# Stored remainders of the projection weights, and three split out-projection tiles used once more at each change of pass

## The chip, the cores and the metric

One Trainium2 chip, of which the program uses one core. The metric is the device time of one execution in microseconds (us), and less is better. Times are given beside the rows of the profile they come from. The engines are named as in the profile: PE (TensorE, matrix products), PEld (its weight loads), DVE (VectorE), ACT (ScalarE), POOL (GpSimd) and SP (SyncE, which issues most of the DMAs).

## What is computed

One layer of a hybrid decoder on 1024 tokens of width 1024, in float32:

```python
def reference(x, ...):
    h = rms_norm(x, norm_mix)                       # (1024, 1024)
    proj = h @ w_in                                 # 1024 -> 8 x 1024
    xa, ga, q, f, v, g, m_a, m_b = split(proj)
    y_a = rg_lru(conv(xa), ...) * gelu(ga)          # recurrence over time
    y_b = rms_norm(hgrn2(q, f, v), hg_norm) * silu(g)   # 8 heads, chunked
    y = sigmoid(m_a) * y_a + sigmoid(m_b) * y_b
    x = x + y @ w_out                               # out-projection, 1024 -> 1024
    h = rms_norm(x, norm_mlp)
    x = x + square(relu(h @ w_up)) @ w_down         # 1024 -> 4096 -> 1024
    return rms_norm(x, norm_final)
```

## The kernel before

**Products in three passes.** The operands of the large products are kept as two float32r tiles, a high part H (the value cast to float32r) and a remainder L (the value minus H). `mm3` (lines 131 to 136) issues three matmuls for each product: H by H, H by L and L by H. For a weight tile, `split` (lines 87 to 90) makes both parts: ACT casts `raw` to `wH` (line 89), then DVE subtracts and writes `wL` (line 90).

**How a weight tile gets to PE.** `seq` is a list, made ahead, of all weight tiles in the order in which PE uses them. Each is 128x1024 floats, 512 KB. `load_w` has SP load tile i into one of 4 `raw` buffers (line 97); `split_w` takes two of the 6 buffers with the tag `w` (three pairs H and L), so that a new pair can only be written when PE is through with a pair used earlier. `next_w` hands out the next tile and has two more split ahead of it (`ahead=2`).

**Mixer projections (about 10 to 550 us).** The 1024 tokens are worked through in two halves of 512 (`c` = 0 and 1), and in each half in 4 pairs of heads (`p` = 0 to 3): 8 stages. A stage uses 9 tiles of weights (two each for v, xa and q, two for f, one, called rg, for the gates of the recurrence). The same 36 tiles of w_in and of the gates are thus loaded and split once in the first half and once more in the second: `pair_tiles` has 72 entries. Between the projections PE computes the chunked attention of the pair before (`hgrn`): scores `sc`, transposes `pk` of the keys `kk`, products `pkv`, and outputs `po`. The order of PE in this part is fixed by the program (`pin`); DVE and ACT are ordered by a scheduler that the framework runs when the program is built, in which `tc.high_priority` moves the splits ahead.

**Gates (about 550 to 835 us).** The four gate projections for all tokens, each as one Strassen-like product of 7 steps. Nothing here is touched.

**Out-projection (about 835 to 930 us).** w_out is 8 tiles: 0 to 3 for output columns 0 to 511 (`hf` = 0), 4 to 7 for columns 512 to 1023 (`hf` = 1). It is gone through three times: `out_proj(0, ...)` for the first 512 tokens, 24 matmuls a tile and four in `pp`; then the loop `for part in range(2)` for the next two lots of 256 tokens, 12 matmuls a tile. So `seq` holds the 8 tiles three times. In the same time the second norm runs (`second_norm`): for each of 8 blocks of 128 tokens ACT squares and sums a row block (line 155), DVE adds (line 156), POOL takes the power (line 157), DVE scales to `xn_h` (line 158), PE transposes it (`xT_h`, line 1203), ACT copies it back (line 1204), and ACT and DVE split the operands `h2...` of the MLP. Late in it, `first_weights` and the code behind it load and split the first weights of the MLP (`q`, `s`, `wA`, `ws10`, `wA120`, `ws30`). The last pass is pinned on PE, and the first MLP products (`uX`) stand between its last transposes.

**MLP (about 930 us to the end).** Untouched.

The names that the prediction uses: `raw<-wts_in` is the load of a weight tile, `wH<-raw` its cast on ACT, `wL<-raw,wH` its subtraction on DVE; `kk<-kk,seg` is the last DVE step before the transposes `pk`; `pv` is the product with v, whose two weight tiles the loop `v_steps` uses by turns from its first token block on; `x2s<-po,x2s` adds a finished out-projection block to the residual.

Of the kernel before, what the change touches and what calls it, by code (L numbers as in the profile page):

```python
# [10 lines left out]
F32 = mybir.dt.float32  # L11
# [7 lines left out]
P = 128  # L19
# [3 lines left out]
NC = S // T  # L23
# [8 lines left out]
MIX_TILES = NPAIR * N_PAIR_TILES  # L32
OUT_TILES = 8
# [13 lines left out]
def trunk(ctx: ExitStack, tc: tile.TileContext, x, wts, mlp, pv, gains, mask_f, mask_u, out):  # L47
    nc = tc.nc
    V, A, G, PE = nc.vector, nc.scalar, nc.gpsimd, nc.tensor
# [4 lines left out]
    dram = ctx.enter_context(tc.tile_pool(name="dram", bufs=1, space=DRAM))  # L54
# [8 lines left out]
    def bank(tag, name):  # L63
        return ps.tile([P, 512], F32, tag=tag, name=name, bufs={"pj": 4, "sc": 2, "hg": 2}[tag])


    pair_tiles = []
    for i in range(NC * NPAIR):
        at = (0, 1, 2, 3, 4, 6, 5)
# [3 lines left out]
    seq = [wts[i] for i in pair_tiles]  # L73
    seq += [mlp[2 * QUADS + q, h] for q in range(2) for h in range(2)]
    n_mix = len(seq)
    for c in range(NC + 1):
        seq += [wts[MIX_TILES + j] for j in range(OUT_TILES)]
    most = [n_mix]
    ready, made = {}, [0]


    in_order = [True]
# [1 line left out]
    def keep(ins):  # L84
        if in_order[0]:
            tc.keep_in_program_order(ins)

    def split(src, h, lo):
        keep(A.copy(h, src))  # L89
        keep(V.tensor_tensor(out=lo, in0=src, in1=h.bitcast(F32), op=ALU.subtract))  # L90
# [4 lines left out]
    def load_w(i):  # L95
        raw = raw_tile(f"raw{i}")
        nc.sync.dma_start(raw, seq[i])
        return raw

    def split_w(i, raw):  # L100
        h = wp.tile([P, 1024], F32R, tag="w", name=f"wH{i}", bufs=6)
        lo = wp.tile([P, 1024], F32R, tag="w", name=f"wL{i}", bufs=6)
        with tc.high_priority(400):
            split(raw, h, lo)
        return h, lo

    raws = []

    def fill_w(n):
        while made[0] < min(n, most[0]):  # L110
            i = made[0]
            raw = raws.pop(0) if raws else load_w(i)
            ready[made[0]] = split_w(i, raw)
            made[0] += 1

    def get_w(i, ahead=2):
        fill_w(i + ahead + 1)
        return ready.pop(i)

    used = [0]  # L120

    def next_w():
        used[0] += 1
        return get_w(used[0] - 1)

    pinned = [False]

    def pin(ins):
        if pinned[0]:
            tc.keep_in_program_order(ins)  # L130

    def mm3(o, ah, al, bh, bl, first, last, goes_on=False):
        how = {"skip_group_check": True} if goes_on else {}
        pin(PE.matmul(o, ah, bh, start=first, stop=False, **how))  # L134
        pin(PE.matmul(o, ah, bl, start=False, stop=False, **how))  # L135
        pin(PE.matmul(o, al, bh, start=False, stop=last, **how))  # L136
# [293 lines left out]

    def rg_lru(c, p, got, xc, xh, xl):
        wh, wl = next_w()
        nm = f"{c}{p}"
        w, ig, e = (mt(t, f"{t}{nm}", (P, 2, T)) for t in ("rw", "ri", "rr"))
# [394 lines left out]
    def last_stage():  # L829
# [27 lines left out]
        on_T(NC - 1, NPAIR - 1, gots[-1])  # L857
        nc.scalar.dma_start(g2d[:, 2:4, :], g2[1])

    def out_proj(c, ykt, res, done):  # L860
        for hf in range(2):
            pp = [bank("pj", f"po{c}{hf}{tt}") for tt in range(4)]
            for j in range(4):
                wh, wl = next_w()
                for k in range(2):
                    ku = 2 * j + k
                    yh, yl = ykt(c, ku)
                    cols = slice(k * 512, (k + 1) * 512)
                    for tt in range(4):
                        cut = slice(tt * P, (tt + 1) * P)  # L870
                        mm3(pp[tt], yh[:, cut], yl[:, cut], wh[:, cols], wl[:, cols], ku == 0, ku == 7)
            for tt in range(4):
                xs = res(tt, hf)
                V.tensor_tensor(out=xs, in0=pp[tt], in1=xs, op=ALU.add)
                done(tt, hf, xs)
# [12 lines left out]
    for i in range(NC * NPAIR):  # L888
        rest = stage(i + 1) if i + 1 < NC * NPAIR else last_stage()
# [231 lines left out]
    for q in own:  # L1121
        n = q + 1
# [103 lines left out]
    rest = []  # L1226
# [21 lines left out]
    def first_weights():  # L1248
        for q in (0, 1):
            load_quad(q)  # L1250
            work[q] = quad_steps(q, (w1p, wp))
            work[q]["a"]()
            if q == 0:
                work[0]["sums"]()
                work[0]["b"]()

    for part in range(2):
        tts = (2 * part, 2 * part + 1)
        for tt in tts:
            x2s[tt] = n2p.tile([P, D], F32, tag="x2", name=f"x2s{tt}", bufs=2)  # L1260
            nc.sync.dma_start(x2s[tt], x[(4 + tt) * P : (5 + tt) * P, :])
            second_norm(tt, 0)
        for hf in range(2):
            pp = {tt: bank("pj", f"po1{hf}{tt}") for tt in tts}
            turn = [(j, tts) for j in range(4)]
            if (part, hf) == (1, 1):
                turn = turn[:2] + [(j, tts[i : i + 1]) for i in range(2) for j in (2, 3)]
                pinned[0] = True
            w = {}
            for n, (j, those) in enumerate(turn):  # L1270
                if j not in w:
                    w[j] = next_w()
                if n == 4:
                    first_weights()
                wh, wl = w[j]
                for k in range(2):
                    ku = 2 * j + k
                    yh, yl = ykt1(part, ku)
                    cols = slice(k * 512, (k + 1) * 512)
                    for tt in those:  # L1280
                        cut = slice((tt % 2) * P, (tt % 2 + 1) * P)
                        mm3(pp[tt], yh[:, cut], yl[:, cut], wh[:, cols], wl[:, cols], ku == 0, ku == 7)
            for tt in tts:
                cols = slice(hf * 512, (hf + 1) * 512)
                V.tensor_tensor(out=x2s[tt][:, cols], in0=pp[tt], in1=x2s[tt][:, cols], op=ALU.add)
        for i, tt in enumerate(tts):
            if part:
                product(i, 0)
            nc.sync.dma_start(x2d[4 + tt], x2s[tt])
            rest.append(second_norm(tt, 1))  # L1290
# [65 lines left out]
    for q in range(1, QUADS):  # L1356
        n = q + 1 if q + 1 < QUADS else QUADS + QUADS - 2
# [71 lines left out]
    for kb in range(n_kb):  # L1429
        last = kb + 1 == n_kb  # L1430
        qs = order[2 * kb : 2 * kb + 2]
        for half in range(2):
# [8 lines left out]
            for step, (bk, wo, uo), prs in [  # L1441
# [105 lines left out]
```

## Time and profile before

| | |
|---|---|
| device time, median of 3 runs | 1564.0 us (1563.96 to 1564.34) |
| profiled execution: its own time | 1564.07 us |
| its span, first to last instruction | 1562.2 us |
| granted TensorE clock, mean over the span | 0.998 |
| PE busy | 1523.0 us (97% of the span), 9072 matmuls |
| DVE busy | 1205.4 us (77%) |
| ACT busy | 818.5 us (52%) |
| DMA | 280.07 MB, mean 179 GB/s |

The profiled execution's own time is the span and 1.9 us around it, and it stands 0.07 us above the median of the runs. Busy time of PE is the union of matmuls whose ends are modelled, so that 97% doesn't say how near PE is to its peak; the waits of PE are to be read from the view of waits and from the distance between the starts of matmuls in the timeline.

### The profile page before, as it was taken

The page shows a single profiled execution, that of the slowest core. Times are in us where ns is not written, and L with a number is a line of the kernel's source. Part 1 is how long each engine was busy: PE and PEld are TensorE (multiplying, and loading weights), DVE is VectorE, ACT ScalarE, POOL GpSimd, SP SyncE. Part 2 cuts the span into 40 slices and gives each one's busy share as a digit, 9 for nine tenths or more (in the row PEclk, how much of TensorE's full clock was granted, in tenths as well). Part 3 has the DMA queues.
Part 4 walks back from the last instruction along what each step waited for, and adds up shares of the span by engine and source line. Part 5 has one row for each costly group of instructions (what it writes and reads, how often), then busy time and mean ns, then how long its engine had stood idle before and what let it go on. Part 6 is the DMA issues. An engine that isn't in the chain of part 4 may idle for free.

```text
span 1562.2 us, 23154 instructions
## 1 busy us (share of the span) xinstructions
PE 1523.0 (97%) x9072; PEld 1271.9 (81%) x9072; DVE 1205.4 (77%) x1706; ACT 818.5 (52%) x1341; POOL 155.5 (10%) x187
## 2 busy tenths in 40 slices
PE   7999999999999999999999989999999999999998
PEld 6878888888788887888888777888888878888886
DVE  5798596696786928786856589888888988888877
ACT  5657757557467435454533376777777631111113
POOL 1013110233624600000000000000000000000000
PEclk9999999999999999999999999999999999999999
DMA  6233233233442274432338862766666675666642
GB/s 235 97 105 109 68 109 108 79 122 120 141 136 95 95 289 181 137 135 81 135 108 308 283 216 99 298 252 250 245 243 242 226 286 225 252 253 253 252 192 108
DMA packets 75341, 280.07 MB, mean 179 GB/s; under 512 B 7776, under 2 KB 20192, under 8 KB 62304
## 3 DMA queue, kind: packets, MB, share of 16 engines
q1 hardware_dynamic: 72208, 267.58, 46.6%
q10 hardware_dynamic: 3024, 11.01, 1.9%
q8 instruction: 71, 1.16, 0.3%
q14 instruction: 38, 0.31, 0.1%
HBM read 193.63 MB, written 84.93 MB: 178 GB/s over the span
## 4 chain that ended last, share of the span: by engine, by line
PE 79%; DVE 11%; ACT 6%; issue 2%; DMA 2%; POOL 0%; DVEq 0%; SPq 0%; ACTq 0%; POOLq 0%
PE dX L134 4%; PE dX L135 4%; PE dX L136 4%; PE uX L134 3%; PE uX L135 3%; PE uX L136 3%; PE gX L134 3%; PE gX L135 3%; PE gX L136 3%; PE dY L135 2%; PE dY L136 2%; PE dY L134 2%; PE uY L134 2%; PE uY L135 2%; PE uY L136 2%
## 5 line engine op out<-in xcount | busy, mean ns | idle before, releaser
L90 DVE TENSOR_TENSOR wL<-raw,wH 128x1024 fp32r<-128x1024 f32 x100 | 123.9, 1240 | 76.2 <-ACT wH L89 75.8
L89 ACT CAST wH<-raw 128x1024 fp32r<-128x1024 f32 x100 | 104.9, 1049 | 78.7 <-PE po L135 26.2
L1456 DVE TENSOR_TENSOR acc<-acc,dX 128x512 f32<-128x512 f32 x128 | 85.1, 685 | 29.2 <-PE dX L136 28.9
L89 ACT CAST wA<-q 128x512 fp32r<-128x512 f32 x46 | 28.5, 621 | 139.1 <-PE dX L136 101.0
L1456 DVE TENSOR_TENSOR acc<-acc,dY 128x512 f32<-128x512 f32 x64 | 43.5, 686 | 15.7 <-PE dY L136 14.5
L136 PE MATMUL po<-wH,y 128*128 128x512 f32 x128 | 50.0, 391 | 0.0
L134 PE MATMUL po<-wH,y 128*128 128x512 f32 x128 | 50.0, 391 | 0.0
L135 PE MATMUL po<-wL,y 128*128 128x512 f32 x128 | 50.0, 391 | 0.0
L1321 ACT ACTIVATE b<-b 128x512 f32<-128x512 f32 x48 | 30.1, 630 | 29.5 <-DVE b L1320 29.4
L157 POOL TENSOR_TENSOR rstd_h<-rstd_h,mhalf 128x1 f32<-128x1 f32 x8 | 5.6, 700 | 379.0 <-DVE rstd_h L156 379.0
L90 DVE TENSOR_TENSOR wA<-q,wA 128x512 fp32r<-128x512 f32 x46 | 31.6, 687 | 13.6 <-ACT wA L89 13.6
L413 DVE SCALAR_TENSOR_TENSOR xc<-xp,pvt,xc 128x512 f32<-128x512 f32 x48 | 40.4, 862 | 0.0
L927 DVE TENSOR_TENSOR s<-q,q 128x512 f32<-128x512 f32 x46 | 31.6, 689 | 2.8 <-DMA q<-mlp_in 2.3
L326 POOL TENSOR_TENSOR stt<-r,stt 128x256 fp32r<-128x256 f32 x16 | 21.1, 1337 | 118.5 <-ACT stt L325 113.5
L932 DVE TENSOR_TENSOR s<-q 128x512 f32<-128x512 f32 x46 | 31.6, 688 | 0.3
L716 ACT ACTIVATE on<-po 128x128 f32<-128x128 f32 x64 | 16.9, 281 | 27.9 <-PE po L712 27.9
L1322 ACT ACTIVATE b<-b 128x512 f32<-128x512 f32 x48 | 30.0, 630 | 1.1
L136 PEld LDWEIGHTS po<-wH,y 128*128 128x128 f32 x128 | 24.1, 188 | 4.9
L135 PEld LDWEIGHTS po<-wL,y 128*128 128x128 f32 x128 | 24.0, 188 | 4.9
L134 PEld LDWEIGHTS po<-wH,y 128*128 128x128 f32 x128 | 24.0, 188 | 4.8
L615 ACT COPY kk<-kc 128x512 f32<-128x512 f32 x8 | 5.0, 622 | 43.1 <-DVE kc L508 43.1
L622 POOL TENSOR_SCALAR scT<-dd 32x256 f32<-32x256 f32 x32 | 21.5, 671 | 52.7 <-DVE dd L537 36.1
(2528 smaller groups left out, 5418.6 us busy)
## 6 DMA issues: line engine op xcount, KB each, us to landing
raw<-wts_in SPq DMA_DIRECT2D x96, 512.0 KB, 3.6
q<-mlp_in SPq DMA_DIRECT2D x92, 512.0 KB, 3.6
x<-x_in SPq DMA_DIRECT2D x8, 512.0 KB, 6.0
hd<-ri SPq DMA_DIRECT2D x16, 256.0 KB, 3.0
od<-onT ACTq DMA_DIRECT2D x8, 512.0 KB, 5.6
cdT<-stT SPq DMA_DIRECT2D x16, 256.0 KB, 3.6
o<-od SPq DMA_DIRECT2D x4, 1024.0 KB, 7.0
h<-hd SPq DMA_DIRECT2D x4, 1024.0 KB, 4.8
```

Source lines behind the costliest of these rows:

```text
L89: keep(A.copy(h, src))
L90: keep(V.tensor_tensor(out=lo, in0=src, in1=h.bitcast(F32), op=ALU.subtract))
L134: pin(PE.matmul(o, ah, bh, start=first, stop=False, **how))
L135: pin(PE.matmul(o, ah, bl, start=False, stop=False, **how))
L136: pin(PE.matmul(o, al, bh, start=False, stop=last, **how))
L413: ins = V.scalar_tensor_tensor(xc[:, s, :], xp[:, j : j + T], pvt[:, PV_CW + 8 * j + u : PV_CW + 8 * j + u + 1], xc[:, s, :], op0=ALU.mult ...
L622: G.tensor_scalar(scT[32 * b : 32 * b + 32, :, 32 * b : 32 * b + 32], dd[32 * b : 32 * b + 32, :, :], 1.0, 0.0, op0=ALU.mult, op1=ALU.add,)
L927: V.tensor_tensor(out=sa[:, 0, :], in0=a21, in1=a22, op=ALU.add)
L932: V.tensor_tensor(out=sb[:, 0, :], in0=a21, in1=a11, op=ALU.add)
L1321: A.activation(b[:, at, :], b[:, at, :], AF.Relu, scale=-1.0 if at == 2 else 1.0)
L1322: A.activation(b[:, at, :], b[:, at, :], AF.Square)
L1456: V.tensor_tensor(out=dst, in0=dst, in1=banks[bk, pr], op=op)
```

## The change

Two edits, which share the code that hands out weight tiles.

First, remainders are kept. When a projection tile that is used again later (`at in pair_tiles[i + 1 :]`) has been split, SP stores its `wL` in DRAM (`rests`). At the second use, ACT casts `raw` to `wH` as before, but `wL` isn't computed: SP loads it from DRAM. That is 36 stores and 36 loads of 512 KB more, and 36 subtractions on DVE fewer.

Second, at each change of pass of the out-projection the last three tiles stay in their buffers and are used once more. `seq` holds 8, 5 and 5 tiles instead of three times 8. `out_proj(0)` ends with tiles 4 to 7; the first lot of 256 tokens starts with columns 512 to 1023 and uses 5, 6 and 7 as they lie, then 4, which is loaded and split again; then come tiles 0 to 3. The second lot uses 1, 2 and 3 as they lie, then 0 again, and then 4 to 7. The parameter `ahead` is cut towards the end of a pass, so that no kept tile is overwritten. That is 6 loads, casts and subtractions fewer.

```diff
-    for c in range(NC + 1):
-        seq += [wts[MIX_TILES + j] for j in range(OUT_TILES)]
+    for new in (range(8), (4, 0, 1, 2, 3), (0, 4, 5, 6, 7)):
+        seq += [wts[MIX_TILES + j] for j in new]
...
     def split_w(i, raw):
         h = wp.tile([P, 1024], F32R, tag="w", name=f"wH{i}", bufs=6)
         lo = wp.tile([P, 1024], F32R, tag="w", name=f"wL{i}", bufs=6)
+        at = pair_tiles[i] if i < len(pair_tiles) else None
         with tc.high_priority(400):
+            if at in rests:
+                A.copy(h, raw)
+                nc.sync.dma_start(lo.bitcast(F32), rests[at])
+                return h, lo
             split(raw, h, lo)
+        if at is not None and at in pair_tiles[i + 1 :]:
+            rests[at] = dram.tile([P, 1024], F32, tag=f"rest{at}", name=f"rest{at}")
+            nc.sync.dma_start(rests[at], lo.bitcast(F32))
         return h, lo
...
-    def next_w():
+    def next_w(ahead=2):
         used[0] += 1
-        return get_w(used[0] - 1)
+        return get_w(used[0] - 1, ahead)
...
     def out_proj(c, ykt, res, done):
         for hf in range(2):
             pp = [bank("pj", f"po{c}{hf}{tt}") for tt in range(4)]
             for j in range(4):
-                wh, wl = next_w()
+                w_kept[j] = wh, wl = next_w(2 if hf == 0 else min(2, 3 - j))
...
-        for hf in range(2):
+        for hf in (1 - part, part):
             pp = {tt: bank("pj", f"po1{hf}{tt}") for tt in tts}
-            turn = [(j, tts) for j in range(4)]
+            kept = hf != part
+            turn = [(j, tts) for j in ((1, 2, 3, 0) if kept else range(4))]
...
-            w = {}
+            w = w_kept
+            if not kept:
+                w.clear()
+            else:
+                del w[0]
             for n, (j, those) in enumerate(turn):
                 if j not in w:
-                    w[j] = next_w()
+                    w[j] = next_w(2 if kept or part else min(2, 3 - j))
+                elif kept:
+                    fill_w(used[0] + n)
```

The scheduler's order changes with it. On DVE, in the first stage of the second half, behind the steps on the scores (`dd`) and ahead of the keys (`kk`), there stood before:

```order
L508 TENSOR_TENSOR qf_3688<-qb_3310,seg_3303 128x16x32
L537 COPY_PREDICATED dd_3301<-mu,sc_10_3611 128x32x2
L413 SCALAR_TENSOR_TENSOR xc_3528<-xp_3532,pvt,xc_3528 128x512
L90 TENSOR_TENSOR wL_3718<-raw_3715,wH_3717 128x1024
L537 COPY_PREDICATED dd_3301<-mu,sc_10_3644 128x8x24
L90 TENSOR_TENSOR xcL_3742<-xc_3528,xcH_3741 128x1024
L537 COPY_PREDICATED dd_3301<-mu,sc_10_3644 128x8x16
L487 SCALAR_TENSOR_TENSOR q_3757<-sq_3758,par,pj_q_0_3591 128x256x2
L90 TENSOR_TENSOR wL_3768<-raw_3765,wH_3767 128x1024
L487 SCALAR_TENSOR_TENSOR q_3757<-sq_3758,par,pj_q_1_3592 128x256x2
L508 TENSOR_TENSOR kk_3293<-kk_3293,seg_3303 128x8x64
```

And now, at the same place on DVE:

```order
L516 TENSOR_TENSOR qf_3760<-qb_3382,seg_3375 128x16x32
L545 COPY_PREDICATED dd_3373<-mu,sc_10_3683 128x32x2
L90 TENSOR_TENSOR xcL_3814<-xc_3600,xcH_3813 128x1024
L545 COPY_PREDICATED dd_3373<-mu,sc_10_3716 128x8x24
L545 COPY_PREDICATED dd_3373<-mu,sc_10_3716 128x8x16
L495 SCALAR_TENSOR_TENSOR q_3829<-sq_3830,par,pj_q_0_3663 128x256x2
L495 SCALAR_TENSOR_TENSOR q_3829<-sq_3830,par,pj_q_1_3664 128x256x2
L516 TENSOR_TENSOR kk_3365<-kk_3365,seg_3375 128x8x64
```

The two weight subtractions are gone, and the last step of the convolution (`xc`) has moved further up.

On SP, at the change from the first half to the second, only loads of `raw` and two stores `hd` stood in a row before:

```order
L97 DMA raw_3104<-wts_in 128x1024
L97 DMA raw_3195<-wts_in 128x1024
L474 DMA hd_96<-ri_2548 128x512 x2
L97 DMA raw_3216<-wts_in 128x1024
L97 DMA raw_3329<-wts_in 128x1024
```

Now a load of a remainder stands between the loads of `raw`; `wL_3291` is the second tile of v of the second half's first stage:

```order
L107 DMA wL_3179<-rest_568 128x1024
L97 DMA raw_3407<-wts_in 128x1024
L107 DMA wL_3270<-rest_157 128x1024
L97 DMA raw_3540<-wts_in 128x1024
L107 DMA wL_3291<-rest_183 128x1024
L97 DMA raw_3570<-wts_in 128x1024
L107 DMA wL_3404<-rest_600 128x1024
```

Each remainder's load waits on SP until PE has freed the buffer that it writes, and the loads of `raw` behind it wait with it.

On DVE, at the end of the out-projection, from the MLP's first weights (`ws10L`) to the scaling of the next-to-last block (`xn_h<-x2s`, by line 158 before and line 166 now), there stood before:

```order
L90 TENSOR_TENSOR ws10L<-s_8802,ws10H 128x1024
L1285 TENSOR_TENSOR x2s_8617<-po_8745,x2s_8617 128x512
L90 TENSOR_TENSOR wA120L<-q_8796,wA120H 128x1024
L1285 TENSOR_TENSOR x2s_8643<-po_8746,x2s_8643 128x512
L156 TENSOR_SCALAR rstd_h_8848<-rstd_h_8848 128x1
L1214 TENSOR_TENSOR xn_h_8576<-xn_h_8576 128x512
L90 TENSOR_TENSOR ws30L<-s_8803,ws30H 128x1024
L90 TENSOR_TENSOR wA_8816<-q_8812,wA_8816 128x512
L158 SCALAR_TENSOR_TENSOR xn_h_8847<-x2s_8617,rstd_h_8848,gain_8355 128x1024
```

And now:

```order
L90 TENSOR_TENSOR ws10L<-s_8838,ws10H 128x1024
L1303 TENSOR_TENSOR x2s_8659<-po_8781,x2s_8659 128x512
L90 TENSOR_TENSOR h2t1L<-xn_h_8461,h2t1H 128x4x128
L90 TENSOR_TENSOR wA120L<-q_8832,wA120H 128x1024
L90 TENSOR_TENSOR wA_8852<-q_8848,wA_8852 128x512
L90 TENSOR_TENSOR ws30L<-s_8839,ws30H 128x1024
L1303 TENSOR_TENSOR x2s_8685<-po_8782,x2s_8685 128x512
L164 TENSOR_SCALAR rstd_h_8884<-rstd_h_8884 128x1
L1225 SCALAR_TENSOR_TENSOR xn_h_8618<-xn_h_8435,xn_h_8618 128x512
L166 SCALAR_TENSOR_TENSOR xn_h_8883<-x2s_8659,rstd_h_8884,gain_8415 128x1024
```

Three splits of MLP weights and one operand (`h2t1L`) now stand ahead of the statistic (`rstd_h`) of that block, where one split stood ahead of it and two between it and the scaling before. PE's order is the same in all mixer stages of the second half; of the transposes `xT_h` five pairs stand 2 to 10 matmuls of the out-projection earlier.

More of the change, by code (lines that the diff above doesn't have):

```diff
@@ L75, in trunk @@
     n_mix = len(seq)
-    for c in range(NC + 1):
-        seq += [wts[MIX_TILES + j] for j in range(OUT_TILES)]
+    for new in (range(8), (4, 0, 1, 2, 3), (0, 4, 5, 6, 7)):
+        seq += [wts[MIX_TILES + j] for j in new]
     most = [n_mix]
-    ready, made = {}, [0]
+    ready, made, rests = {}, [0], {}
     in_order = [True]
@@ L858, in last_stage @@
         nc.scalar.dma_start(g2d[:, 2:4, :], g2[1])
+    w_kept = {}
     def out_proj(c, ykt, res, done):
@@ L1281, in trunk @@
                         cut = slice((tt % 2) * P, (tt % 2 + 1) * P)
-                        mm3(pp[tt], yh[:, cut], yl[:, cut], wh[:, cols], wl[:, cols], ku == 0, ku == 7)
+                        last = j == (0 if kept else 3) and k == 1
+                        mm3(pp[tt], yh[:, cut], yl[:, cut], wh[:, cols], wl[:, cols], j == kept and k == 0, last)
             for tt in tts:
```

## The prediction

> **What bounds the kernel now.** I read the page first, then the waits of PE by stretch, then the timelines of PE and DVE around the longest of these waits, and last the DMAs.
>
> ```profile
> span 1562.2 us, 23154 instructions
> PE 1523.0 (97%) x9072; PEld 1271.9 (81%) x9072; DVE 1205.4 (77%) x1706; ACT 818.5 (52%) x1341; POOL 155.5 (10%) x187
> L90 DVE TENSOR_TENSOR wL<-raw,wH 128x1024 fp32r<-128x1024 f32 x100 | 123.9, 1240 | 76.2 <-ACT wH L89 75.8
> ```
>
> PE is busy nearly all the time, and the change takes no matmul away. DVE spends 123.9 us in the 100 subtractions, but waits 76.2 us ahead of them, nearly all for ACT's cast. So DVE time that is saved becomes time of the kernel only where PE waits for DVE. Four stretches show where that is; the columns are busy time of PE, PEld, DVE, ACT and POOL, then PE's clock, the DMA share and GB/s:
>
> ```profile
> 33.00:300.00 267.00, 263.86 (x2306) 226.24 (x2305) 206.60 (x379) 165.72 (x312) 36.52 (x50) 1.00 0.30 101
> 300.00:580.00 280.00, 274.28 (x2381) 235.96 (x2380) 203.31 (x309) 168.53 (x347) 108.30 (x113) 1.00 0.40 138
> 880.00:950.00 70.00, 62.03 (x292) 49.61 (x290) 59.48 (x82) 47.64 (x77) 5.60 (x8) 0.98 0.59 203
> 937.30:942.00 4.70, 4.62 (x18) 3.84 (x19) 4.26 (x7) 2.73 (x5) 0.86 (x1) 0.64 0.14 32
> ```
>
> The first is the first half of the mixer, where the stores are; the second is the second half, with the remainder loads; the third is the end of the out-projection, where PE stands still for 8 of 70 us; the last, inside the third, is the only place of them where PE's clock is lowered. The waits of PE over 1 us in each, first half, second half and out-projection (total, times, longest):
>
> ```profile
> PE po L709 <- DVE sn L695: 1.4, 1, 1.4
> ```
>
> ```profile
> PE pk L674 <- DVE kk L508: 5.3, 3, 1.8
> ```
>
> ```profile
> PE xT_h L1203 <- DVE rstd_h L156: 3.0, 2, 2.4
> PE xT_h L1203 <- DVE xn_h L158: 2.0, 1, 2.0
> PE xT_h L1203 <- ACT h2B21H L89: 1.4, 1, 1.4
> PE xT_h L1203 <- ACT wH L89: 1.1, 1, 1.1
> ```
>
> So 36 subtractions less in the second half can give 5.3 us there at most, not the 36 x 1.27 = 45.7 us that DVE works on them:
>
> ```profile
> L90 DVE TENSOR_TENSOR wL<-raw,wH 128x1024 fp32r<-128x1024 f32 x36 | 45.7, 1269 | 25.2 <-ACT wH L89 25.2
> ```
>
> **The change, part by part.**
>
> *Stores in the first half: 0.* 36 stores of 512 KB on SP, read from a `wL` that PE keeps in use anyway, at a DMA share of 0.30. SP's next loads stand behind a store, which waits for `wL`; before, the next load of `raw` waited for the same subtraction, since that frees its buffer:
>
> ```profile
> SPq L97 <- DVE wL L90: 216.5, 52, 11.7
> ```
>
> So the queue waits no longer than it did. DVE loses nothing in this half, and its wait of 1.4 us stays. If this cover is gone, a store (3.4 us, as the loads below) would hold up the next `raw`, which is two tiles ahead of its use; I take 0, with up to +1 us for the range.
>
> *Subtractions in the second half: -5.3 us.* The first of the three waits is this (DVE and PE in the order of time, start and duration; the wait in brackets):
>
> ```profile
> 347.41 1.75 DVE L90 TENSOR_TENSOR wL<-raw,wH 128x1024 fp32r<-128x1024 f32 x1
> 351.60 1.22 DVE L90 TENSOR_TENSOR wL<-raw,wH 128x1024 fp32r<-128x1024 f32 x1
> 352.74 0.74 DVE L487 SCALAR_TENSOR_TENSOR q<-sq,par,pj_q 128x512 f32<-128x512 f32 x1
> 353.40 0.68 DVE L508 TENSOR_TENSOR kk<-kk,seg 128x512 f32<-128x512 f32 x1
> ```
>
> ```profile
> 351.95 0.39 PE L136 MATMUL pj_f<-hT10H,wL 128*128 128x512 f32 x1
> 354.14 0.88 PE L674 MATMUL pk<-ident,kk 128*128 128x128 f32 x6 [1.79 <-DVE kk L508]
> ```
>
> PE is through with its projection at 352.34 and starts the transposes at 354.14, when `kk` is done. DVE works without a break before it, and its new order (shown above) has neither of the two subtractions ahead of `kk`. The next instruction starts 1.67 us after the start of the first and 1.14 us after that of the second, so `kk` comes 2.8 us earlier by these two alone, more than the 1.79 us that PE waits. The other two waits stand at the same step of the next stages and are no longer (1.8 is the longest), with subtractions of their stage ahead as well. All three go: -5.3. What is late next is ACT or the scores, which have never been last here; that is a rival.
>
> *Remainder loads in the second half: 0, with a bound above.* `wL` can't be read before PE has freed its buffer, and SP, behind it the next loads of `raw`, waits for that. Before, DVE's subtraction waited for the same buffer. Only the time from release to first use changes: it held 1.27 us of DVE, and now holds a load. I went through all 36: most have 12 to 19 us from the last matmul that reads the buffer to the first that reads the new remainder, four (second tile of xa) have 7.1 us, and four have the least, the second tile of v. There, in the first stage:
>
> ```profile
> 303.20 0.39 PE L136 MATMUL pi<-xcH,wL 128*128 128x512 f32 x1
> 309.06 0.28 PE L135 MATMUL pv<-wL,hT11H 128*128 128x256 f32 x1
> ```
>
> The release is at 303.20 + 0.39 = 303.59, the use at 309.06: 5.47 us. Loads of the same size on the same queue in that stretch land so (minimum, median, maximum of 37), and the longest that the page has for 512 KB on this queue is the second row (median of 8):
>
> ```profile
> DMA to landing us min/median/max: 3.1/3.4/6.6
> ```
>
> ```profile
> y<-yd SPq DMA_DIRECT2D x8, 512.0 KB, 8.5
> ```
>
> At the median 5.47 - 3.4 = 2.1 us are left, so I take 0. At the maximum a stage loses 6.6 - 5.47 = 1.1 us, four of them 4.5; at 8.5 us the rival below results. Below nothing the cost can't go, since the subtraction's place is counted already. The DMA share of 0.40 rises by 18.9 MB in 280 us, 67 GB/s on 138, so to about 0.40 x 205 / 138 = 0.6, what the end of the out-projection has already (0.59): queues get longer, and I put the loads nearer to the median than to the maximum.
>
> *Kept tiles in the out-projection: -1.5 us.* Six casts, subtractions and loads less. Of the waits of PE there, 2.0 us are for `xn_h` and 1.1 for `wH`, at the first blocks, which follow the load of `x2a` and of the tiles; these transfers are still there, and I count nothing. The next two:
>
> ```profile
> 908.61 1.06 PE L1203 MATMUL xT_h<-ident,xn_h 128*128 128x128 f32 x8 [0.64 <-DVE rstd_h L156]
> 918.25 1.06 PE L1203 MATMUL xT_h<-ident,xn_h 128*128 128x128 f32 x8 [1.44 <-ACT h2B21H L89]
> ```
>
> ```profile
> 914.50 1.22 DVE L90 TENSOR_TENSOR wL<-raw,wH 128x1024 fp32r<-128x1024 f32 x1
> 915.64 0.15 DVE L156 TENSOR_SCALAR rstd_h<-rstd_h 128x1 f32<-128x1 f32 x1
> ```
>
> At the second, `rstd_h`, from which POOL, `xn_h` and the transposes follow, has to wait on DVE for a subtraction of a tile that is now kept: 1.14 us earlier, and the casts beside it are fewer by as much: -1.4. At the first I count most of 0.64: -0.5. Against that stands the last one:
>
> ```profile
> 933.55 0.14 DVE L156 TENSOR_SCALAR rstd_h<-rstd_h 128x1 f32<-128x1 f32 x1
> 934.21 1.22 DVE L90 TENSOR_TENSOR ws30L<-s,ws30H 128x1024 fp32r<-128x1024 f32 x1
> 935.95 1.28 DVE L158 SCALAR_TENSOR_TENSOR xn_h<-x2s,rstd_h,gain 128x1024 f32<-128x1024 f32 x1
> ```
>
> ```profile
> 934.60 0.39 PE L136 MATMUL uX<-h2B11H,wA 128*128 128x512 f32 x1
> 937.38 1.06 PE L1203 MATMUL xT_h<-ident,xn_h 128*128 128x128 f32 x8 [2.39 <-DVE rstd_h L156]
> 938.65 0.63 PE L135 MATMUL uX<-h2B11L,wA 128*128 128x512 f32 x1
> 939.07 0.63 PE L136 MATMUL uX<-h2B11H,wA 128*128 128x512 f32 x1
> ```
>
> Here the new order puts `wA120L`, `wA`, `ws30L` and `h2t1L` ahead of `rstd_h`, where before two of these splits filled the time that POOL took. If all of them came on top, this would be 1.22 + 0.69 us more; if the six subtractions less let the whole tail start earlier, nothing or a gain. I take +0.4, nearer to the gain, since DVE has 6 x 1.2 us less before it. Sum of the part: -0.5 - 1.4 + 0.4 = -1.5, between -4.5 and +2.5.
>
> This last wait has a second price. PE's clock falls behind it: the matmuls at 938.65 and 939.07 start 0.42 us apart, and over 4.70 us the clock is 0.64, which costs 0.36 x 4.70 = 1.7 us. I leave it as it is. The Trainium skill ("TensorE: Matmul & The Clock Gate", section "HAM oscillation — how this bites in real kernels") gives about 3.4 us as the idle time from which the clock drops. The gap here is 2.39 us and the clock drops all the same, so the row decides; by the page alone the gap would have no second price, and a shorter gap would only give back its own length.
>
> *Sum.* The profiled execution took 1564.07 us, 1562.2 of span and 1.9 around it, 0.07 above the median of the runs. 1564.07 + 0 - 5.3 + 0 - 1.5 = 1557.3, less the 0.07: 1557.2 us.
>
> **The rivals.**
>
> *The tail gets easier, about 1553 us.* With DVE 7 us freer the last gap falls from 2.39 us to a few tenths and the clock stays up: the 0.4 is not lost, about 2 more are gained, and 1.7 of the clock: 1557.2 - 4.1 = 1553.1. For it speaks the work taken away, against it the order on DVE.
>
> *Another wait takes the place of `kk`, about 1562.5 us.* If ACT's part of `q` and `kk`, or the scores, come at 354 us anyway, the 5.3 stay: 1557.2 + 5.3 = 1562.5. Against it: DVE has work ready all through that stretch and starts `q` and `kk` right behind the subtraction.
>
> *The tail gets worse, about 1563 us.* Fewer tiles stand ready at the changes of pass, and tiles 4 and 0 are fetched again right behind kept ones. If one of them is late so that another gap of some 2.4 us brings the clock down again, 2.4 + 1.7 come on top, and the 1.5 isn't gained: 1557.2 + 5.6 = 1562.8.
>
> *Slower: the remainder of the second v tile lands late, about 1570 us.* If these loads, queued among loads of `raw`, take as long as `y<-yd`, PE waits at the `pv` with `wL` 8.5 + 0.1 - 5.47 = 3.1 us in each of four stages, 12.5 in all: 1569.7. It makes the kernel slower once the loss passes 6.8 us, 1.7 us a stage, so from a landing of 7.1 us on. For it: more traffic, and SP issues the load only at the release. Against it: no load of `raw` there took over 6.6.
>
> **How the numbers follow.** The forecast, 1555.5 to 1559.5, gets 0.52: both its terms rest on rows. The easier tail gets 0.15, the other wait 0.10, the worse tail 0.11, the late remainders 0.12. About 0.2%, 3.1 us, is what a measurement of this kernel can tell from no change; that puts the bounds at 1560.9 and 1567.1. Faster: 0.52 + 0.15 = 0.67, and 0.01 of the worse tail where it is small; same: 0.10 + 0.09; slower: 0.12 and 0.01 of the worse tail. The range, from the easier tail less 1 us to beyond both cases of no change, 1552 to 1564.5, leaves out the late remainders and the ends of the others, not quite 0.2.
>
> **What would show it.** Right: in the new profile PE has no wait for `kk` in the second half, the second `pv` has no wait for a DMA, remainders land in under 5.3 us, the waits of `xT_h` sum to some 6 us, and the clock is still lowered once behind the last. Wrong: a wait of PE for a DMA at `pv` or `pi` (late remainders), for ACT at `pk` (another wait), or a second stretch with a lowered clock between 880 and 950 (worse tail).

## The result and the profile after

The changed kernel takes 1562.5 us at the median of 11 runs (1559.7 to 1564.6) against 1564.4 us before (11 runs, 1562.0 to 1566.9): a ratio of 0.9984, 95% interval 0.9976 to 0.9991. By this ratio it is 2.5 us faster (1.4 to 3.8; the medians lie 1.9 us apart), where 6.8 us were forecast. The time lies in the forecast range and the sign is right, but the gain is little more than a third of the forecast.

Both kernels spread by 5 us between executions, so the one execution that a profile shows can stand 2 us off. Below, times of kernels are told by ratios over many runs, and causes by single traces. The profiled execution after took 1560.6 us. Its page:

```profile
span 1558.8 us, 23239 instructions
PE 1523.1 (98%) x9072; PEld 1273.4 (82%) x9072; DVE 1159.8 (74%) x1664; ACT 813.4 (52%) x1335; POOL 152.0 (10%) x187
L90 DVE TENSOR_TENSOR wL<-raw,wH 128x1024 fp32r<-128x1024 f32 x58 | 71.1, 1225 | 46.7 <-ACT wH L89 46.7
raw<-wts_in SPq DMA_DIRECT2D x90, 512.0 KB, 4.7
rest<-wL SPq DMA_DIRECT2D x36, 512.0 KB, 2.9
wL<-rest SPq DMA_DIRECT2D x36, 512.0 KB, 4.3
```

42 subtractions are gone (100 to 58), and DVE is busy 45.6 us less. The same three stretches as in the prediction, by the same columns:

```profile
33.00:300.00 267.00, 261.76 (x2295) 224.29 (x2294) 198.28 (x371) 165.70 (x310) 36.67 (x49) 1.00 0.51 179
300.00:580.00 280.00, 277.23 (x2395) 238.86 (x2394) 174.13 (x282) 169.50 (x352) 104.69 (x114) 1.00 0.55 190
880.00:950.00 70.00, 62.55 (x299) 49.88 (x298) 59.03 (x84) 45.67 (x76) 6.14 (x8) 1.00 0.50 169
```

The first stretch has 2.1 us less of PE than before (263.86), at a DMA share of 0.51 instead of 0.30; the second has 3.0 us more. The waits of PE from 240 to 580 us, where before there were only the three for `kk` (5.3 us):

```profile
PE sc L526 <- issue: 1.5, 1, 1.5
PE sc L526 <- DVE qb L516: 1.3, 1, 1.3
PE pk L682 <- DVE kk L516: 0.8, 1, 0.8
PE sc L656 <- DVE qf L516: 0.2, 1, 0.2
```

The three are gone, and others have come: one that waits for nothing the profile shows (`issue`), and three in the last stage of the mixer (522 to 541 us). So in these two executions the gates start almost where they did, 0.37 us earlier:

```profile
564.74 0.48 PE L134 MATMUL gX<-hT00H,wA 128*128 128x512 f32 x1
```

```profile
564.37 0.48 PE L142 MATMUL gX<-hT00H,wA 128*128 128x512 f32 x1
```

By the starts of the same matmuls in the two traces, PE is 0.8 us later than before at 240 us, 1.8 us more behind the stop at 275 us (`issue`), then 5.4 us earlier by 500 us, where the three waits were, and 2.4 us later again in the last stage of the mixer. That adds up to 0.4 us earlier.

At the end of the out-projection (880 to 950 us) PE now waits:

```profile
PE xT_h L1213 <- DVE rstd_h L164: 3.7, 3, 2.9
PE xT_h L1213 <- DVE xn_h L166: 1.4, 2, 1.0
PE uX L143 <- DVE h2n2L L90: 0.7, 1, 0.7
PE uY L143 <- DVE h2t1L L90: 0.6, 1, 0.6
PE xT_h L1213 <- ACT h2B11H L89: 0.5, 1, 0.5
```

The waits of `xT_h` sum to 5.6 us instead of 7.5, the longest has grown from 2.4 to 2.9, and in this execution PE's clock wasn't lowered behind it (1.00 in the stretch).

### The profile page after: what moved, and what is told of

Its sections match the earlier page's. It is cut to its first block, busy times and chain, and to the rows that moved or that the text cites. A ratio compares the mean times of both kernels' runs of the same rounds, so it can differ in the third digit from the quotient of the medians.

```text
span 1558.8 us, 23239 instructions
## 1 busy us (share of the span) xinstructions
PE 1523.1 (98%) x9072; PEld 1273.4 (82%) x9072; DVE 1159.8 (74%) x1664; ACT 813.4 (52%) x1335; POOL 152.0 (10%) x187
## 3 DMA queue, kind: packets, MB, share of 16 engines
q8 instruction: 71, 1.16, 0.3%
## 4 chain that ended last, share of the span: by engine, by line
PE 81%; DVE 9%; ACT 5%; DMA 2%; issue 2%; POOL 0%; DVEq 0%; POOLq 0%; SPq 0%; ACTq 0%
PE dX L142 4%; PE dX L143 4%; PE dX L144 4%; PE uX L142 3%; PE uX L144 3%; PE uX L143 3%; PE gX L142 3%; PE gX L144 3%; PE gX L143 3%; PE pj_q L142 2%; PE dY L144 2%; PE dY L142 2%; PE dY L143 2%; PE pj_q L143 2%; PE pj_xa L143 2%
## 5 line engine op out<-in xcount | busy, mean ns | idle before, releaser
L90 DVE TENSOR_TENSOR wL<-raw,wH 128x1024 fp32r<-128x1024 f32 x58 | 71.1, 1225 | 46.7 <-ACT wH L89 46.7
L89 ACT CAST wH<-raw 128x1024 fp32r<-128x1024 f32 x58 | 60.9, 1050 | 64.5 <-PE po L143 23.9
L106 ACT CAST wH<-raw 128x1024 fp32r<-128x1024 f32 x36 | 37.7, 1048 | 18.9 <-issue 10.6
L334 POOL TENSOR_TENSOR stt<-r,stt 128x256 fp32r<-128x256 f32 x16 | 14.7, 940 | 124.3 <-ACT stt L333 112.0
L516 DVE TENSOR_TENSOR seg<-seg 128x128 f32<-128x128 f32 (+2 forms) x96 | 25.0, 309 | 0.4
```

The lines of the kernel that those rows point to most:

```text
L106: A.copy(h, raw)
```

## The experiments

The ratios, each against the kernel before on the same chip, with the number of runs of the experiment:

| kernel | remainders | kept tiles | `s<-q` moved | ratio, 95% interval | runs |
|---|---|---|---|---|---|
| changed kernel | 36 | yes | no | 0.9984 (0.9976 to 0.9991) | 11 |
| e1 | 36 | no | no | 0.9986 (0.9978 to 0.9995) | 11 |
| e2 | none | yes | no | 1.0000 (0.9991 to 1.0009) | 11 |
| e3 | 6, tiles of f | yes | no | 0.9985 (0.9976 to 0.9994) | 11 |
| e4 | 36 stored, none loaded | yes | no | 0.9997 (0.9988 to 1.0006) | 10 |
| e5 | 27, last three pairs | yes | no | 0.9966 (0.9956 to 0.9976) | 8 |
| e10 | as e5 | yes | no | 0.9961 (0.9948 to 0.9973) | 5 |
| e9 | as e5 | no | no | 0.9974 (0.9966 to 0.9983) | 11 |
| e13 | 36 stored, 27 loaded | yes | no | 0.9966 (0.9956 to 0.9976) | 11 |
| e8 | as e5 | yes | yes | 0.9958 (0.9945 to 0.9972) | 5 |
| e12 | 36 | yes | yes | 0.9968 (0.9956 to 0.9980) | 5 |
| e14 | as e5 | no | yes | 0.9969 (0.9957 to 0.9980) | 6 |
| e11 | none | no | yes | 0.9996 (0.9987 to 1.0005) | 11 |
| e15 | none | yes | yes | 0.9990 (0.9981 to 0.9998) | 11 |

One thousandth is 1.56 us.

**Each edit alone, six remainders, and stores alone.** The first two undo one edit each. The third and the fourth are the changed kernel with

```diff
-        if at is not None and at in pair_tiles[i + 1 :]:
+        if at in (14, 15, 23, 24, 32, 33) and at in pair_tiles[i + 1 :]:   # e3
```

```diff
-            if at in rests:                                                # e4
-                A.copy(h, raw)
-                nc.sync.dma_start(lo.bitcast(F32), rests[at])
-                return h, lo
```

> The remainders alone; the out-projection loads and splits its tiles three times, as before. Theory G (given back inside the mixer): the three waits for kk are gone (5.3 us), but PE loses about 2 to 2.5 us in stalls inside the runs of score matmuls at the end of the first half (275 us) and about 3 us at the last stage of the second half (522 to 541 us), so that this kernel is within 1.5 us of the one before; its first gate matmuls (gX) start no more than 1 us earlier than before. Theory S (the seam takes it): the mixer keeps its 5.3 us, so this kernel is 4 to 6 us faster than before, and the missing 4 us are a loss of the kept tiles.

> The kept out-projection tiles alone; the mixer subtracts all 72 times, as before. Theory G: 1.5 to 3 us faster than before, all of it between 880 and 950 us, the three waits for kk (5.3 us) still there. Theory S: 2 us or more slower than before.

> As the changed kernel, but only the two tiles of f of the last three head pairs have their remainder stored and loaded (6 stores and 6 loads instead of 36 and 36), which are the two subtractions that stood ahead of kk. Theory G with the stall at 275 us laid to the traffic of remainders (PE's instructions fetched late): the stall is gone as no remainder is under way there, the waits for kk are gone too, the loss at the last stage stays: 1.5 to 2.5 us faster than the changed kernel, 4 to 5 us faster than before. If the stall at 275 us has nothing to do with that traffic, it stays and the time is that of the changed kernel within 1 us. If all nine subtractions of a stage have to go for kk to come in time, the waits of 5.3 us come back and the kernel is 3 us or more slower than the changed one.

> As the changed kernel, but the stored remainders are not loaded: the second half subtracts as before. Theory G with the stall laid to the loads: no stall at 275 us, stalls of the first half under 0.7 us each, the waits for kk back; about the time of the kept tiles alone, within 1 us. If the stores make the stalls, those of the first half stay (1.5 us and more at 275 us) and the kernel is 2 us slower than the kept tiles alone.

Neither theory came out whole. As far as can be told the gain is all from the remainders (e1), and it is 2.2 us, neither 5.3 nor nothing. The kept tiles alone gave nothing that can be measured (e2), no loss either. What the traces show of PE's waits in the mixer is clearer than the times. With the remainders alone (e1), 240 to 580 us, and its clock behind the longer of the two stalls:

```profile
PE sc L526 <- issue: 2.7, 2, 2.3
```

```profile
279.00:283.00 4.00, 3.81 (x21) 3.03 (x21) 3.24 (x7) 1.24 (x2) 0.00 (x0) 0.57 0.03 8
```

The stall inside the scores is 2.3 us here, and the clock stays at 0.57 over the 4 us behind it, 0.43 x 4 = 1.7 us more. With six remainders (e3), with stores alone (e4) and without remainders (e2) there is no such stall.

Six remainders halve the waits for `kk` and don't remove them: PE's stops there are 1.0 to 1.1 us instead of 1.9 by the distance of its matmuls. DVE at the first of them:

```profile
350.51 0.75 DVE L495 SCALAR_TENSOR_TENSOR q<-sq,par,pj_q 128x512 f32<-128x512 f32 x1 [0.69 <-ACT sq L493]
351.94 0.75 DVE L495 SCALAR_TENSOR_TENSOR q<-sq,par,pj_q 128x512 f32<-128x512 f32 x1 [0.69 <-ACT sq L493]
352.61 0.69 DVE L516 TENSOR_TENSOR kk<-kk,seg 128x512 f32<-128x512 f32 x1
```

`kk` starts 0.79 us earlier than before (353.40), not 2.8: with the two subtractions gone, DVE waits twice for ACT's `sq`. With the earlier subtractions of the stage gone too, as in the changed kernel, DVE has no such wait there.

**Which remainders make the stall.** e5 neither stores nor loads those of the first pair, e13 stores them and doesn't load them, and e6 loads all and subtracts all the same.

```diff
-        if at is not None and at in pair_tiles[i + 1 :]:
+        if at is not None and at > 8 and at in pair_tiles[i + 1 :]:        # e5, e9, e10
```

```diff
-            if at in rests:
+            if at in rests and at > 8:                                     # e13
```

```diff
-                A.copy(h, raw)
                 nc.sync.dma_start(lo.bitcast(F32), rests[at])
+                split(raw, h, lo)                                          # e6
                 return h, lo
```

> As the changed kernel, but the remainders of the nine tiles of the first head pair are neither stored nor loaded (27 stores and 27 loads are left), so that no remainder is loaded between about 245 and 300 us. Theory F (PE's instructions are fetched late because the loads of remainders fill the DMA engines): no stall inside the score matmuls near 275 us (it was 1.72 us with all remainders, 2.45 us with the remainders alone); the three waits for kk are gone; so 1.5 to 2.5 us faster than the changed kernel on the mean, 1560 to 1561 us. Theory N (the stall comes from another order or timing of the changed program, not from the loads): it stays, and the time is the changed kernel's within 1 us.

> As the changed kernel, but each tile whose remainder is loaded is subtracted again all the same, over the loaded one: all the traffic and none of the DVE time saved. Theory F: the stalls near 150 and 275 us are there (1.5 us or more at 275), and the waits for kk too (5 us or more), so about 1566.5 us, 2 us or more over the kernel with the stores alone (mean 1564.3). Theory N: no stall over 0.5 us near 275, the time within 1 us of the stores alone.

> The remainders of the last three head pairs with the kept tiles once more, on the chip of this comparison: 1558 to 1560 us on the mean, no stall at 275 us, as in its first run.

> As the changed kernel with all 36 remainders stored, but those of the first head pair's nine tiles are not loaded again: 27 loads. If the loads delay the instruction fetch at 275 us: no stall there, 1558 to 1559.3 us on the mean as with 27 of both; a stall near 150 us, under the stores, of up to 1 us may stay. If the stores do it: the stall at 275 us stays, 1561.5 to 1562.5 us.

e5, e10 and e13 are the main result: nine loads less, and the kernel gains another 2.8 to 3.6 us on the changed one. Without the kept tiles the same nine loads make 1.9 us (e1 against e9), with the sums `s<-q` moved 1.6 us (e12 against e8). e13 stores as much as the changed kernel, so it is the loads that cost. Its trace is of the slowest of its eleven executions (1562.4 us), and the gain can't be read from it. How the loads cost is seen at the scores at 275 us. PE in the changed kernel:

```profile
275.14 0.78 PE L526 MATMUL sc<-qb,kc 128*32 128x48 f32 x52
277.43 0.25 PE L526 MATMUL sc<-qb,kc 128*32 128x48 f32 x5 [1.52 <-issue]
```

PE stops in the middle of 64 equal matmuls, and the profile shows no semaphore that it waits for. The view of the DMA queues of that kernel from 275.09 to 276.04 us:

```profile
q1 hardware_dynamic: 87, 0.29, 78.1%
q8 instruction: 1, 0.02, 6.1%
```

One packet of the queue of instructions is carried here, in the trace from 275.10 to 276.03 us; it ends 1.6 us after the scores began at 274.43 (`sc<-qa,kb`). In e5 the scores begin at 273.87, and the like packet is carried before them:

```profile
273.87 0.89 PE L526 MATMUL sc<-qa,kb 128*32 128x48 f32 x64
274.57 0.88 PE L526 MATMUL sc<-qb,kc 128*32 128x48 f32 x64
```

Its end against the start of the scores, in all kernels at this place: before -0.5 us, e3 -0.4, e4 -0.2, e5 -0.6, e13 -0.9, the other nine -0.4 to -0.7, no stall; e12 +0.6, a stall of 0.8; changed kernel +1.6, stall 1.7; e1 +2.5, stall 2.4 (stalls by the distance of the matmuls). The same pairing holds elsewhere: in the 17 traces PE stops 16 times inside a run of score matmuls of the mixer (over 0.25 us from start to start), and each time a packet of this queue ends 1.3 to 1.6 us before PE goes on, though a trace has only 71 such packets. The DMA share over the 6 us around 270 to 276, before (269 to 275), e5, e13 and the changed kernel:

```profile
269.00:275.00 6.00, 6.00 (x209) 4.74 (x207) 5.93 (x16) 3.37 (x5) 0.80 (x2) 1.00 0.55 188
```

```profile
270.00:276.00 6.00, 6.00 (x208) 4.91 (x208) 5.64 (x16) 2.90 (x5) 0.54 (x2) 1.00 0.55 196
```

```profile
270.00:276.00 6.00, 6.00 (x208) 4.78 (x207) 5.93 (x16) 3.08 (x5) 0.73 (x2) 1.00 0.59 214
```

```profile
270.00:276.00 6.00, 5.91 (x196) 4.55 (x195) 4.08 (x8) 3.37 (x5) 0.00 (x0) 1.00 0.86 308
```

So the loads fill the DMA engines to 0.86, PE's next instructions come late, and PE stands. The request for the packet isn't in the trace, so that it waits in a DMA engine behind the loads is inferred; that it ends late where the loads are, and PE stalls by about as much, is shown. The stall is 0.8 to 2.4 us, and in e1 the lowered clock costs 1.7 us more; where the rest of the 1.6 to 3.6 us goes isn't located. Smaller stalls of the same kind stay near 150 us, at the stores (0 to 1.35 us), and near 460 us, at other loads (0 to 1.25 us). The DMA share there, 0.99 from 144 to 150.5 us and 0.98 from 452 to 459 in the changed kernel, was 0.59 and 0.58 before. It alone doesn't decide: the stores alone (e4) have 0.99 at 150 us and no stall.

e6 doesn't settle the question: its ratio is 1.0197 (1.0181 to 1.0213, 4 runs), because the subtraction now had to wait for the load that it overwrites, and PE waited for DVE (first row from 240 to 580 us, second from 300 to 580):

```profile
DVE wL L90 <- DMA wL<-rest: 28.8, 13, 4.6
PE po L717 <- DVE sn L703: 20.6, 3, 6.9
```

It had no stall at 275 us, at a DMA share of 0.74 there (270 to 276 us): its loads are spread by these waits.

**The last stage of the mixer.** e7 moves the sums that POOL makes there one stage ahead; e8, e11, e12, e14 and e15 move the two DVE sums `s<-q`.

```diff
-        if i > 4:
+        if i > 3:
             combos_on(2)
...
         yield from v_of(NC * NPAIR)
-        combos_on(2)                                                       # e7
```

```diff
         with tc.high_priority(600):
             gwork[q]["a"]()
-            if q == own[0]:
+        if q == own[0]:
+            with tc.high_priority(300):
                 gwork[q]["sums"]()
                 gwork[q]["b"]()                                            # e8, e11, e12, e14, e15
```

> The kernel before, with the sums that POOL makes for the Strassen operands (r, stt, stT) moved one stage ahead, so that POOL has one group instead of three in the last stage of the mixer. Theory P (the loss of some 2.4 us at 522 to 541 us, which is there in one execution and not in another with the same mixer program, comes from POOL's sums running beside DVE's chain qb, dd, kk): no such loss in the trace, and a mean 1 to 1.5 us below the kernel before, with less spread between executions. Rival: the sums only slow DVE in an earlier stage instead; the time is that of before within 0.5 us, or 1 to 3 us slower with longer waits for kk.

> The kernel with the remainders of the last three head pairs, and in the last stage of the mixer the two sums s<-q of the first gate weights moved on DVE from between the steps qb to behind them. Theory P (in some executions DVE pauses 0.4 to 0.8 us there for the load of q; POOL's sums get in, and until their end DVE's small steps take 0.95 us instead of 0.43, so that PE waits some 2.4 us for qb, qf and kk): no pause, POOL's first stt takes over 6 us, no wait of PE in the last stage; 1.5 to 2.5 us faster than the same kernel without the move (mean 1558.8), about 1556.5 to 1557. Rival: POOL gets in at another place all the same: within 0.7 us of it, the waits still there.

> The kernel before with the two sums s<-q moved behind qb and nothing else. Theory P: the loss in the last stage, which the kernel before has in a part of its executions, can't come; the mean falls by the part that had it, 0.5 to 2 us, and the spread with it. Rival: the kernel before never had the loss (its one trace shows none): the mean stays within 0.4 us.

> The changed kernel with the two sums s<-q of the last mixer stage moved behind qb. Theory P (the changed kernel gives back some 2.4 us in the last stage): no wait of PE there, a mean of 1560 to 1560.8 us against 1562.3 without the move; the stall at 275 us stays. Rival (the loss is covered by something later): 1562 us, within 0.7 of the changed kernel.

e7 was slower (1.0021, 1.0009 to 1.0033, 12 runs): the waits moved with the sums. Its waits from 240 to 580 us, beside those for `kk`, are at 282 to 285 us, and behind them the clock is at half for 6.8 us:

```profile
PE sc L648 <- DVE qf L508: 1.6, 1, 1.6
PE sc L637 <- DVE qb L508: 1.5, 1, 1.5
```

What happens in the last stage is read from DVE and POOL together. Changed kernel:

```profile
513.47 1.27 DVE L937 TENSOR_TENSOR s<-q,q 128x512 f32<-128x512 f32 x1 [0.56 <-issue]
514.66 0.97 DVE L516 TENSOR_TENSOR qb<-qa,seg 128x256 f32<-128x256 f32 x1
510.83 3.37 POOL L334 TENSOR_TENSOR stt<-r,stt 128x256 fp32r<-128x256 f32 x2 [20.05 <-ACT stt L333]
```

Before:

```profile
516.21 0.43 DVE L508 TENSOR_TENSOR qb<-qa,seg 128x256 f32<-128x256 f32 x1
513.62 7.89 POOL L326 TENSOR_TENSOR stt<-r,stt 128x256 fp32r<-128x256 f32 x2 [20.74 <-ACT stt L325]
```

e2, whose mixer is instruction for instruction that of before:

```profile
516.66 1.05 DVE L929 TENSOR_TENSOR s<-q,q 128x512 f32<-128x512 f32 x1 [0.79 <-DMA q<-mlp_in]
517.64 0.95 DVE L508 TENSOR_TENSOR qb<-qa,seg 128x256 f32<-128x256 f32 x1
513.78 3.38 POOL L326 TENSOR_TENSOR stt<-r,stt 128x256 fp32r<-128x256 f32 x2 [20.71 <-ACT stt L325]
```

The same `qb` takes 0.43 or 0.95 us, and POOL's pair of sums 7.9 or 3.4: the two engines get in each other's way, and either one or the other pays. Which one pays turns on a pause of DVE: where it waits for the load of `q`, 0.1 us (e10, e13) to 0.8 us (e2), POOL gets in, and DVE's small steps take twice as long for the next 7 us. In all traces without the move in which PE came to this stage early, 2.4 to 4.7 us ahead of before (changed kernel, e3, e5, e9, e10, e13), the load of `q` wasn't there when DVE was, and PE then lost about 2 us to `qb`, `qf` and `kk`. Of those that came to it no earlier than before, e2 lost it, before, e1 and e4 didn't. The Trainium skill ("SBUF — State Buffer", section "SBUF: two separate sides") says that DVE and GpSimd share a pair of ports under an exclusive lock, that for a DVE step with two inputs in SBUF against a GpSimd step that reads SBUF whichever starts first holds it for its instruction, and that the other blocks. The rows fit that, with 0.43 against 0.95 us for the same step; that this lock is the cause is not shown by a run of its own.

With the sums moved behind `qb`, e8 has no pause, POOL's pair takes 6.70 us, and of PE's waits from 240 to 580 us only an instruction stall is left:

```profile
509.43 6.70 POOL L334 TENSOR_TENSOR stt<-r,stt 128x256 fp32r<-128x256 f32 x2 [20.32 <-ACT stt L333]
```

```profile
PE sc L526 <- issue: 1.0, 1, 1.0
```

The mechanism is shown; its worth on the whole is less even. On the changed kernel the move gives 1.6 thousandths, 2.5 us (e12). On 27 remainders with the kept tiles it gives 0.3 to 0.8 thousandths (e8 against e10 and e5), without them 0.5 (e14 against e9), on the kernel before 0.4, with the kept tiles alone 1.0 (e15 against e2): all of one sign, each within its interval. In the traces the last stage costs PE 2.1 to 2.5 us where the loss comes, and 0.1 us or less with the move; why less than 2 us of that arrives in the times isn't settled.

**The kept tiles once more**, in three more pairs of kernels:

> The remainders of the last three head pairs without the kept out-projection tiles. Theory K0 (the kept tiles are worth nothing on the mean, as in the run of them alone): within 0.7 us of the same kernel with the kept tiles. Theory K1 (they are worth the 1.0 to 1.5 us that the single traces of the out-projection show): 1 to 1.5 us slower than it.

> 27 remainders, the sums s<-q moved behind qb, no kept tiles. If the kept tiles are worth 1 us or more, 1 us or more above the same kernel with them (mean 1557.6); if nothing, within 0.6 us of it. If the move is worth 2 us, 2 us below the same kernel without it (mean 1560.0).

> The kept tiles alone with the sums s<-q moved behind qb, no remainders. Against the move alone (mean 1562.9): 1 us or more faster if the kept tiles are worth what the traces of the out-projection show, within 0.6 us if they are worth nothing.

The ratios differ by 1.1 thousandths between e14 and e8, by 0.6 between e11 and e15, by 1.3 between e9 and e10: 0.9 to 2.0 us for the kept tiles, none of these differences clear of its own interval. The first two pairs gave less, 0.2 (e1 and the changed kernel) and 0.0 (e2); the mean of the five is 0.6, or 1.0 us. From a fixed matmul in the gates to one of the MLP, the traces take 223.7 us in the mean of the six with the old out-projection (standard error 0.3), 222.3 in that of the eleven with the new one (0.35), so 1.4 us less. Nearly half of that is the clock, which happened to be lowered more often in the six (see the end): with the time lost to it taken off, 0.75 us are left, with a standard error of 0.45.

The fastest of the kernels is e8, at a median of 1557.1 us, 0.9958 (0.9945 to 0.9972); e10 isn't told apart from it.

## Why the prediction was right or wrong

- **Stores, 0.** Not told from 0 in the times: stores alone with the kept tiles are at 0.9997 (0.9988 to 1.0006). The traces show a small cost: PE comes to 240 us 0.2 to 1.9 us later than before in the eleven with 27 or 36 stores, 0.8 us in the mean, and -0.1 to 0.4 us later in the others. The stalls near 150 us, up to 1.35 us, are part of it; in some executions it passes the bound that was given (+1).
- **Subtractions, -5.3.** The three waits went, as forecast. The step that failed is the one behind: 'All three go: -5.3' was added to the sum as if nothing else could become late. Two things did: PE's instructions (1.8 us at 275 us), and DVE's own chain in the last stage (2.4 us; both in the changed kernel's trace). Alone, the remainders gave 2.2 us (e1). Also wrong was its ground, that 'these two alone' bring `kk` 2.8 us earlier: they bring 0.79 (e3), since ACT's `sq` is next. The rival 'another wait takes the place of `kk`' had named that, and it is real with six remainders, not with 36.
- **Remainder loads, 0 with a bound above.** The term that was mis-sized. It priced the loads by when they land, and there it was right: they land in time, and PE waits for none of them, although the longest takes 5.8 us, over the 5.3 that was named as a sign.

```profile
DMA to landing us min/median/max: 3.1/4.3/5.8
```

  But it asked only who reads the transfer, not who else uses the DMA engines. Nine of the 36 loads cost 2.8 us (e13 against the changed kernel; their intervals just meet), of which the stall of PE's instructions accounts for 1.7 in the changed kernel's trace. The rising DMA share had been worked out (0.6), yet as a mean over 280 us, and from 300 us on; the loads begin at 247 us, and the place that counted has 0.86 over 6 us.
- **Kept tiles, -1.5.** Near it in the traces (-1.4), but part of that is luck: without the clock it is -0.75, and in the profiled execution the clock wasn't lowered behind the last wait, although that had been expected. It isn't told from zero in the comparison of this edit alone. Inside it the parts fell otherwise: by the distance of the matmuls (less the usual 0.22 us) the stop at 908 us lost 0.1 us, not 0.5, that at 916 us 1.2, not 1.4, and the one at 886 us, where nothing was counted, fell from between 1.25 and 2.2 to between 0.2 and 0.8. The last gap grew from 2.55 to 3.07 us, close to the +0.4.
- **The sum.** The late remainders and the worse tail with a second drop of the clock didn't come. With nine loads less and the sums `s<-q` moved, the kernel takes 1557.1 us, about what was forecast for the changed one: the two losses are the main part of what the forecast lacked. That the numbers meet so closely is partly chance, since the kept tiles gave less and the last stage's 2.4 us arrive only in part.

## What to carry to other kernels

A load that lands in time can still cost: ask what else passes through the DMA engines while it runs, PE's own instructions among them, and look for stops of PE that wait for nothing (`issue`) in runs of small matmuls. Use a trade of traffic for engine time only in the stages whose wait it removes; here the first pair's nine tiles brought nothing and cost 1.6 to 3.6 us. When a wait goes, walk on to the next stage with everything shifted, and check which transfer will then be late.

## What was not expected of the hardware

- Packets of instructions, 16 KB each, are carried by the DMA engines during the execution (queue `q8`, 71 of them, 1.16 MB). With the engines busy at 0.86 and 0.93 over 6 us (changed kernel, e1), a packet that ended 1.6 and 2.5 us after the start of a run of short matmuls stopped PE for 1.7 and 2.4 us.
- DVE and POOL have two lasting ways of sharing: a DVE step of 128x256 takes 0.43 us while POOL's pair takes 6.7 to 7.9, or 0.95 while it takes 3.4 to 3.9. A pause of DVE of 0.1 to 0.8 us turns the one into the other.
- Whether the clock is lowered behind the last gap of the out-projection turns on when the gap comes: with the old gap (2.55 us) it was lowered in five of six traces, with the new (3.07 to 3.27 us) in six of eleven, each time for at least 3.41 us at half speed. In each of the 17 traces all changes of the clock lie whole multiples of 3.413 us apart. It was lowered, 17 times between 30 and 1530 us, at the end of just those periods of this grid in which PE's stops (over 0.5 us, by the distance of the matmuls less 0.22) added up to 2.04 us or more; in no other period at full clock did they reach 2.0. The same gap can lie inside one period, as before (the first two rows, clock 0.50 in the second), or be divided between two, as in the changed kernel (the last two, clock 1.00):

```profile
934.92:938.34 3.42, 1.03 (x10) 0.99 (x10) 2.98 (x6) 1.85 (x5) 0.86 (x1) 1.00 0.55 223
938.34:941.75 3.41, 3.41 (x10) 2.64 (x10) 3.41 (x5) 2.43 (x5) 0.00 (x0) 0.50 0.14 24
```

```profile
930.33:933.74 3.41, 1.72 (x8) 1.10 (x6) 2.98 (x6) 2.68 (x6) 0.85 (x1) 1.00 0.67 270
933.74:937.15 3.41, 2.19 (x14) 2.00 (x15) 2.97 (x5) 1.99 (x4) 0.86 (x1) 1.00 0.24 97
```

  By the rule of the Trainium skill quoted in the prediction ("TensorE: Matmul & The Clock Gate", section "HAM oscillation — how this bites in real kernels") neither gap would lower it; here the rows decide.
